# A hybrid decoder trunk on one core: the two halves of a norm's sum are added before the float32 product, and the planner's figures change

## The chip, the cores and the metric

The kernel runs on one core of a Trainium2 chip. The metric is device time in microseconds of one execution. The engines are named as in the profile: PE (TensorE matmuls), PEld (TensorE weight loads), DVE (VectorE), ACT (ScalarE), POOL (GpSimd) and SP (SyncE, which issues most DMAs).

## The reference, cut to what matters

Two layers act on a residual stream `h` of 528 tokens (16 meta tokens and 512 real ones) and 1024 channels. Each layer has a mixer and an FFN, each between two RMS norms:

```
def rms_norm(x, g):
    xf = x.astype(jnp.float32)
    y = xf * lax.rsqrt(jnp.mean(xf * xf, axis=-1, keepdims=True) + RMS_EPS)
    return (y * g.astype(jnp.float32)).astype(x.dtype)

def layer_norm(x, g, b):
    mu = jnp.mean(xf, axis=-1, keepdims=True)
    var = jnp.mean(jnp.square(xf - mu), axis=-1, keepdims=True)
    y = (xf - mu) * lax.rsqrt(var + LN_EPS)
...
for l in range(DEPTH):
    h = h + rms_norm(mixer(rms_norm(h)))      # attention, Conformer conv, short gated conv
    h = h + rms_norm(ffn(rms_norm(h)))        # up, causal conv, silu gate, down
```

The mixer has eight attention heads with a forget gate, a Conformer module of 256 channels (a causal convolution of 31 taps, a layer norm over its 256 channels, silu, a small product) and a short gated convolution. Their results get a norm per head and go through `w_out`.

## The kernel before, in words

**Layout.** Channels lie on the 128 partitions, tokens along the free dimension. A tensor of 1024 channels is 8 blocks (`KD`) of 128x528, and work goes by halves of 264 tokens (`hf` 0 and 1). In the last layer the first tokens are not needed, so there halves of 250 and 256 tokens occur.

**Products.** A weight is split into two float32r parts, `whi` and `wlo` (a cast on ACT, a subtraction on DVE, 128x1024 each), the activations too (`uhi`, `ulo` or the pairs `y`). `mm3` (L837) makes three products of these parts for each block; it is most of the kernel. The FFN's up projections run through L2288 where seven-term sums are used. Weights stream from DRAM all the time through `raw` tiles.

**Sums over channels.** A norm needs a sum over channels, thus over partitions. This is a product with a constant matrix in true float32: `om_d` (1/1024) for the RMS norms, `om_c` (1/256) for the layer norm, `bd` and `hsel` for the head norms. `Norms.square` squares two blocks at a time (ACT, L925) into a tile of two halves, 128x2x264; further pairs are added into the tile `acc` (DVE, L934). `Norms.factor` (L974) then multiplies `om_d` with each of the two halves and adds them up in PSUM. Some sums are kept apart: with `apart` the last two pairs of a sum are not added to `acc` but go to `om_d` as tiles `c` of their own, and `square_alone` (L950) squares a single block, for the very last norm. After the product come Ln (L984), Exp (L987), a square (L988) on ACT and two steps on DVE (L989, L995) that give the factor. `post_norm` scales the sub-layer's result (L1050), adds it to `h` (L1060) and makes the next activations (L1066 on ACT, L1068 on DVE).

**The layer norm** is in `conv_tail`: `om_c` with the two blocks of the convolution (tiles `cacc`, L1760), the subtraction of the mean, squares into the tiles `apad`, and `om_c` with both of those (L1789). The 31 taps before it (L1153) run on DVE.

**Attention.** For each head, L1593 makes logits for a row maximum, L1600 reduces them on DVE in pieces, L1608 puts the maxima on a diagonal on POOL (five pieces: one of 16 and four of 128), L1617 multiplies by ones, and the result goes into the row of `q` that the real logits (L1637) use. After Exp (ACT, L1644) POOL clears the part above the diagonal (L1651) and L1671 multiplies by the values. L1737 and L1323 are the products of the head norms.

**What sets the order.** In the mixers and in the norm stages (`finish`) a planner, the class `Flow`, deals all instructions out: each operation on ACT, DVE, POOL or SP has a duration (`us`), a priority, a delay until its result is there (`lat`) and the tokens it waits for; `flow.mm` advances TensorE's clock. The operation that can start first in this plan is issued next, so the plan's figures fix the order of each engine's queue; an engine then works through its queue in that order and waits where something is late. `act_us`, `dve_us` and `stt_us` give the durations. The FFN's products between these stages are not dealt out by the planner.

POOL also carries the accumulating DMAs of weight sums (L534), each of which waits for the one before.

Of the kernel before, what the change touches and what calls it, by code (L numbers as in the profile page):

```python
# [21 lines left out]
H = L // 2  # L22
# [339 lines left out]
def mm4_us(n):  # L362

    return max(n / 600 + 0.005, 0.22)


def act_us(n):
    return 0.17 + 0.0009 * n


def dve_us(n):
    return 0.17 + 0.00101 * n


def stt_us(n):
    return 0.22 + 0.00102 * n


def dma_us(n):
# [10 lines left out]
def tile_hybrid_trunk(ctx: ExitStack, tc: tile.TileContext, xT, wflat, pv_d, out):  # L390
# [97 lines left out]
    def half_sl(hf):  # L488
        return slice(H * hf, H * (hf + 1))
# [408 lines left out]
    class Norms:  # L898
# [17 lines left out]
        def square(self, key, k, src, n, *after, prio=1):  # L916

            apart = self.alone.get(key, self.apart.get(key[0], 0))
            s = self.sums.setdefault(key, {"parts": {}})
            us = act_us(2 * n)  # L920
            box, slot = {}, Slot()

            def squares(tile):
                box["c"] = tile()
                nc.scalar.activation(box["c"], src, AF.Square)  # L925

            if k == 0:
                a = act(us, lambda: squares(lambda: T(self.pool, [P, 2, H], F32, "acc", 2)[:, :, :n]), *after,
                        prio=prio, takes=[(self.acc, slot)])
                s["acc"], s["at"] = box, a  # L930
            else:
                a = act(us, lambda: squares(lambda: self.c_tile(n)), *after, prio=prio, takes=[(self.c, slot)])
                if k < KD - 2 * apart:
                    s["at"] = dve(dve_us(2 * n), lambda: nc.vector.tensor_add(s["acc"]["c"], s["acc"]["c"], box["c"]),  # L934
                                  a, s["at"], prio=prio)
# [65 lines left out]

    def gained(h, y, a, z, k, g, after, prio):

        return [act(act_us(z - a) + 0.06, lambda i=i: nc.scalar.activation(
            y[:, k + i, a:z], h[:, k + i, a:z], AF.Copy, scale=g[:, k + i:k + i + 1]), after, prio=prio) for i in range(2)]

    def pre_norm(norms, hf, n, hg, hg_at, out, at, prio):
# [16 lines left out]
    def post_norm(norms, key, nkey, h, h_at, a, z, yp, g, g_next, at, hf, prio, out_at, y_out, on_pe=(), to=None):  # L1024

        n = z - a
        yield from norms.factor(key, n)
        s = norms.sums[key]  # L1030
        sums = {}
        for k in on_pe:
            if k:
                slots = []
                for _ in range(2):
                    slots.append((yield from flow.grab(pring[0]["s"])))
                t = psum[:, 2:4]
            else:
                slots = [(yield from flow.grab(pring[0]["mm"]))]
                t = mmt(slots[0].buf)  # L1040
            for i in range(2):
                nc.tensor.matmul(t[:, i, :n], lhsT=ident, rhs=h[:, k + i, a:z], start=True, stop=False)
            flow.mm(2 * 0.0017 * n)
            sums[k] = t[:, :, :n], slots

        def pair(k, prio):
            y = yp[:, k:k + 2, a:z]
            hk = h[:, k:k + 2, a:z]
            if g is None:
                e = dve(dve_us(2 * n), lambda: nc.vector.tensor_mul(  # L1050
                    y, y, s["r"].unsqueeze(1).to_broadcast([P, 2, n])), s["r_at"], *y_out[hf, k], prio=prio)
            else:
                e = s["r_at"]
                for i in range(2):
                    e = dve(stt_us(n), lambda i=i: nc.vector.scalar_tensor_tensor(
                        y[:, i, :], in0=y[:, i, :], scalar=g[:, k + i:k + i + 1], in1=s["r"],
                        op0=ALU.mult, op1=ALU.mult), e, prio=prio)
            if k in on_pe:
                return e
            f = dve(dve_us(2 * n), lambda: nc.vector.tensor_add(hk, hk, y), e, *h_at, prio=prio)  # L1060
            if g_next is not None:
                at[hf, k] = []
                for i in range(2):
                    hi, lo = (uhi[:, k + i, a:z], ulo[:, k + i, a:z]) if to is None else (to[0][k + i], to[1][k + i])
                    gc = g_next[:, k + i:k + i + 1]
                    c = act(act_us(n) + 0.06, lambda i=i, hi=hi, gc=gc: nc.scalar.activation(  # L1066
                        hi, hk[:, i, :], AF.Copy, scale=gc), f, prio=prio)
                    at[hf, k] += [c, dve(stt_us(n), lambda i=i, hi=hi, lo=lo, gc=gc: nc.vector.scalar_tensor_tensor(  # L1068
                        lo, in0=hk[:, i, :], scalar=gc, in1=hi.bitcast(F32), op0=ALU.mult, op1=ALU.subtract), c, prio=prio)]
            if nkey is not None:  # L1070
                norms.square(nkey, k, hk, n, f, prio=prio)
            out_at[hf, k] = f
            return e

        scaled = [pair(k, prio + 0.01 * k) for k in range(0, KD, 2)]
        s["free"].close(*scaled)
        for k in on_pe:
            yield [scaled[k // 2]]
            t, slots = sums[k]
            for i in range(2):  # L1080
                nc.tensor.matmul(t[:, i], lhsT=ident, rhs=yp[:, k + i, a:z], start=False, stop=True)
# [43 lines left out]
    def mixer(l, ypool, first, close_first, spans, front, rzs, u_at):  # L1125
# [622 lines left out]
        def conv_tail(blk):  # L1748
# [4 lines left out]
            sq = [T(mq, [P, L + CK - 1], F32, "apad", 2) for _ in range(2)]  # L1753
            us, vs = act_us(H), dve_us(H)
            at = {}
            for hf in range(2):
                c = half_sl(hf)
                ps, slot = yield from bank("mm")
                for j in range(2):
                    nc.tensor.matmul(ps[:, :H], lhsT=om_c, rhs=conv[j][:, c], start=j == 0, stop=j == 1)  # L1760
# [10 lines left out]
            def silu(j, c, box, mine, e):  # L1771
# [9 lines left out]
                g = act(us, lambda: nc.scalar.copy(a2[j][0][:, c], n), f)  # L1781
                return dve(vs, lambda: nc.vector.tensor_sub(a2[j][1][:, c], n, a2[j][0][:, c].bitcast(F32)), g)

            for hf in range(2):
                c = half_sl(hf)
                yield [at[hf, 0], at[hf, 1]]
                ps, slot = yield from bank("mm")
                for j in range(2):
                    nc.tensor.matmul(ps[:, :H], lhsT=om_c, rhs=sq[j][:, c], start=j == 0, stop=j == 1)  # L1789
# [69 lines left out]
    def finish(norms, h, h_at, spans, ks, rhs, y_at, yp, gpost, gpre, nsplit, first=None, rz=None, scaled=None,  # L1859
# [13 lines left out]
        def evac(m, hf, src, tok, slot):  # L1873
            a, z = spans[hf]
            d = yp[:, m:m + 2, a:z]
            if merge:
                e = dve(dve_us(2 * n[hf]), lambda: nc.vector.tensor_add(d, d, src), tok, prio=0)
                slot.close(e)
                a = norms.square(("y", hf), m, d, n[hf], e, prio=0)
                y_out[hf, m] = [act(act_us(n[hf]) + 0.06, lambda i=i: nc.scalar.activation(  # L1880
                    d[:, i, :], d[:, i, :], AF.Copy, scale=gpost[:, m + i:m + i + 1]), a, prio=0.6 * hf) for i in range(2)] if GA else []
                return

            es = [act(act_us(n[hf]) + 0.06, lambda i=i: nc.scalar.activation(
                d[:, i, :], src[:, i, :], AF.Copy, scale=gpost[:, m + i:m + i + 1]), tok, prio=0) for i in range(2)]
            slot.close(norms.square(("y", hf), m, src, n[hf], tok, prio=0), *es)
            y_out[hf, m] = es
# [7 lines left out]
        def evac_alone(m, i, src, tok):  # L1895
# [5 lines left out]
            y_out.setdefault((hf, m), []).append(act(act_us(n[hf]) + 0.06, lambda: nc.scalar.activation(  # L1901
                d, d, AF.Copy, scale=gpost[:, m + i:m + i + 1]), b, prio=0.6))
            return e

# [124 lines left out]
    with tc.tile_pool(name="pre", bufs=2, reuse_waits="tile") as sp, tc.manual_schedule(engines=every):  # L2029
# [12 lines left out]
        reads = {}  # L2042
        for k in range(KD):
            hk, hi, lo, gc = h[:, k, :H], u_raw[0][k], u_raw[1][k], g0[:, k:k + 1]
            c = act(act_us(H) + 0.06, lambda hk=hk, hi=hi, gc=gc: nc.scalar.activation(hi, hk, AF.Copy, scale=gc),
                    h_at[0, k - k % 2], prio=0)
            d = dve(stt_us(H), lambda hk=hk, hi=hi, lo=lo, gc=gc: nc.vector.scalar_tensor_tensor(
                lo, in0=hk, scalar=gc, in1=hi.bitcast(F32), op0=ALU.mult, op1=ALU.subtract), c, prio=0)
# [442 lines left out]
```

## Time and profile before

| | us |
|---|---|
| median of 3 runs | 1262.84 |
| lowest and highest run | 1262.09, 1263.26 |
| the profiled execution: span from first to last instruction | 1262.4 |
| PE busy | 1243.7 |
| PEld busy | 1194.0 |
| DVE busy | 926.1 |
| ACT busy | 710.3 |
| POOL busy | 174.6 |

The profiled execution has no time of its own beside its span; the span lies 0.4 us under the median of the runs, which is taken as what lies around it. In a row of groups stand the line, the engine, the operation, out<-in, the count, then busy time and mean duration in ns, then the idle time of the engine just before and what ended it. In a row of the timeline stand the start in us from the span's start, the time taken, and in brackets the idle time before it. A wait row gives who waited for whom, the total in us, the number of times and the longest.

### The profile page before, as it was taken

The numbers are of one execution on the slowest core, as the hardware profiler recorded it, in microseconds if no ns is written. First come the engines' busy times: TensorE is split into PE (matmuls) and PEld (weight loads), VectorE is DVE, ScalarE is ACT, GpSimd is POOL, SyncE is SP. The second block draws the span as 40 slices with busy tenths as digits, with TensorE's granted clock in tenths as the row PEclk, the third lists the DMA queues.
The fourth block names the chain that finished last, engine by engine and source line by source line (L and its number), as shares of the span: only waits on it lengthen the run. The fifth ranks groups of instructions, "written<-read, shape, count | busy, mean of one in ns | idle before, by whom it ended". The sixth has DMA issues, their size and how long they took to land.

```text
span 1262.4 us, 24292 instructions
## 1 busy us (share of the span) xinstructions
PE 1243.7 (99%) x9554; PEld 1194.0 (95%) x9554; DVE 926.1 (73%) x1581; ACT 710.3 (56%) x1377; POOL 174.6 (14%) x360
## 2 busy tenths in 40 slices
PE   8999999999999999999999999999999999999997
PEld 8998898999999999999999988999999899989997
DVE  7887866589874776487688878656799748756964
ACT  7254576655444663476673545775554447526763
POOL 1323411001111001010003244120021000000000
PEclk9999999999999999999999999999999999999999
DMA  7357551726648755776652584547166565465611
GB/s 245 82 155 173 126 119 44 259 87 149 186 147 334 244 193 149 240 195 169 208 189 67 156 194 110 144 111 241 71 163 176 146 218 170 153 223 182 203 60 67
DMA packets 80755, 206.59 MB, mean 164 GB/s; under 512 B 8624, under 2 KB 18992, under 8 KB 80128
## 3 DMA queue, kind: packets, MB, share of 16 engines
q1 hardware_dynamic: 66976, 168.20, 42.1%
q0 software_dynamic: 13664, 36.84, 13.0%
q8 instruction: 75, 1.23, 0.4%
q14 instruction: 40, 0.33, 0.1%
HBM read 170.82 MB, written 50.60 MB: 175 GB/s over the span
## 4 chain that ended last, share of the span: by engine, by line
PE 89%; DVE 3%; issue 3%; DMA 2%; ACT 2%; POOL 1%; SPq 0%; DVEq 0%; POOLq 0%; ACTq 0%
PE psum L837 58%; PE psum L2288 17%; PE psum L1407 5%; PE psum L1671 3%; PE psum L1637 2%; PE psum L974 1%; PE psum L1593 1%; DMA raw<-in_w_dram 1%; PE psum L1737 1%; PE psum L1323 1%; DMA w_split<-slo 0%; DMA h<-in_w_dram 0%; POOL dm L1608 0%; DVE yp L1050 0%; DMA h<-in_x_dram 0%
## 5 line engine op out<-in xcount | busy, mean ns | idle before, releaser
L837 PE MATMUL psum<-y,whi 128*128 128x264 f32 (+3 forms) x1968 | 383.8, 299 | 0.8 <-DVE zs L989 0.7
L837 PEld LDWEIGHTS psum<-y,whi 128*128 128x128 f32 x1968 | 305.6, 188 | 13.8 <-DVE zs L989 0.9
L837 PE MATMUL psum<-uhi,whi 128*128 128x264 f32 (+1 forms) x1168 | 292.1, 289 | 1.5 <-ACT uhi L2069 0.7
L837 PE MATMUL psum<-ulo,whi 128*128 128x264 f32 (+1 forms) x1168 | 285.7, 284 | 0.6 <-DVE ulo L2071 0.4
L837 PE MATMUL psum<-uhi,wlo 128*128 128x264 f32 (+1 forms) x1168 | 285.1, 283 | 0.0
L837 PE MATMUL psum<-y,wlo 128*128 128x264 f32 (+3 forms) x984 | 273.7, 297 | 0.3 <-DVE wlo L793 0.3
L837 PEld LDWEIGHTS psum<-uhi,whi 128*128 128x128 f32 x1168 | 201.5, 188 | 6.2 <-issue 1.6
L837 PEld LDWEIGHTS psum<-ulo,whi 128*128 128x128 f32 x1168 | 201.6, 188 | 1.3 <-DVE ulo L2071 0.6
L837 PEld LDWEIGHTS psum<-uhi,wlo 128*128 128x128 f32 x1168 | 201.3, 188 | 0.0
L837 PEld LDWEIGHTS psum<-y,wlo 128*128 128x128 f32 x984 | 177.8, 188 | 5.8 <-DVE wlo L793 0.6
L2173 DVE SCALAR_TENSOR_TENSOR c<-zs,pv,c 128x528 f32<-128x528 f32 (+1 forms) x176 | 130.6, 756 | 23.5 <-ACT c L2171 22.2
L652 ACT CAST whi<-raw 128x1024 fp32r<-128x1024 f32 (+1 forms) x65 | 66.1, 1020 | 97.1 <-PE psum L837 74.5
L793 DVE TENSOR_TENSOR wlo<-raw,whi 128x1024 fp32r<-128x1024 f32 (+2 forms) x80 | 95.6, 1203 | 29.7 <-ACT whi L789 29.2
L789 ACT CAST whi<-raw 128x1024 fp32r<-128x1024 f32 (+2 forms) x80 | 81.7, 1031 | 24.9 <-PE psum L837 18.0
L653 DVE TENSOR_TENSOR wlo<-raw,whi 128x1024 fp32r<-128x1024 f32 (+1 forms) x65 | 76.9, 1183 | 21.1 <-ACT whi L652 21.0
L1153 DVE SCALAR_TENSOR_TENSOR cacc<-apad,pv,cacc 128x528 f32<-128x528 f32 x120 | 87.6, 772 | 0.1
L2288 PE MATMUL psum<-uhi,whi 128*128 128x258 f32 (+1 forms) x252 | 71.3, 284 | 0.0
L2288 PE MATMUL psum<-ulo,whi 128*128 128x258 f32 (+1 forms) x252 | 71.2, 283 | 0.0
L2288 PE MATMUL psum<-uhi,wlo 128*128 128x258 f32 (+1 forms) x252 | 70.7, 283 | 0.0
L2171 ACT ACTIVATE c<-zs,pv 128x528 f32<-128x528 f32 (+1 forms) x88 | 63.0, 727 | 6.8 <-DVE zs L2136 2.7
L2206 POOL COPY cols<-y 128x1 f32<-128x1 f32 x24 | 17.2, 716 | 335.8 <-ACT y L2187 335.5
L2288 PE MATMUL psum<-t,shi 128*128 128x258 f32 (+1 forms) x336 | 63.2, 283 | 0.0
(273 smaller groups left out, 2323.9 us busy)
## 6 DMA issues: line engine op xcount, KB each, us to landing
raw<-in_w_dram SPq DMA_DIRECT2D x114, 512.0 KB, 4.5
raw<-in_w_dram SPq DMA_DIRECT2D x30, 448.0 KB, 5.1
h<-in_w_dram SPq DMA_DIRECT2D x25, 512.0 KB, 4.5
raw<-w_sum SPq DMA_DIRECT2D x21, 512.0 KB, 5.4
h<-w_sum SPq DMA_DIRECT2D x21, 512.0 KB, 4.8
h<-in_w_dram POOLq DMA_DIRECT2D x16, 512.0 KB, 4.6
w_sum<-h POOLq DMA_DIRECT2D x16, 512.0 KB, 6.4
w_sum<-in_w_dram SPq DMA_DIRECT2D x26, 256.0 KB, 5.2
```

The source lines that it names most:

```text
L652: nc.scalar.copy(hi[:, :sz], raw[:, :sz])
L653: last_low[0] = nc.vector.tensor_sub(lo[:, :sz], raw[:, :sz], hi[:, :sz].bitcast(F32))
L789: nc.scalar.copy(box["hi"][:, :sz], box["raw"][:, :sz])
L793: nc.vector.tensor_sub(lo[:, :sz], box["raw"][:, :sz], box["hi"][:, :sz].bitcast(F32))
L837: nc.tensor.matmul(d, lhsT=w[a][:, k, cols], rhs=rhs(b, k, hf), start=start and i == 0 and p == 0, stop=stop and i == n - 1 and p == 2)
L1153: nc.vector.scalar_tensor_tensor(conv[j], in0=src, in1=conv[j], scalar=col("a_dw_w", CK * j + i), op0=ALU.mult, op1=ALU.add)
L1407: nc.tensor.matmul(ps[:n, :nw], lhsT=(uhi, ulo)[ui][:, k, P * b:P * b + n], rhs=w[wi][:, k % 4, :], start=k == 0 and p == 0, stop=k == KD ...
L1637: nc.tensor.matmul(s, lhsT=k[:, ka:ka + kn], rhs=q[:, s0:qz], start=i == 0, stop=i == 1)
L1671: nc.tensor.matmul(acc[:, s0 - qa:qz - qa], lhsT=vals[:, b].rearrange("p h d -> p (h d)")[:, o:o + P], rhs=box["p"], start=b == 0, stop=b ...
L2171: nc.scalar.activation(dst, src[:, 2:2 + 2 * fw], AF.Copy, scale=wtap(2, t))
L2173: nc.vector.scalar_tensor_tensor(dst, in0=src[:, i:i + 2 * fw], scalar=wtap(i, t), in1=dst, op0=ALU.mult, op1=ALU.add)
L2288: nc.tensor.matmul(psum[:, bank, :n7], lhsT=w[a][:, k0 + k, :], rhs=rhs(b, k), start=start and k == 0 and p == 0, stop=stop and k == K2 - ...
```

## The change

There are two edits. First, `Norms.fold` is new: it adds the second half of a squared tile to the first on DVE, and `factor` then makes one product instead of two; `square` calls it for `acc` and for the parts that are kept apart. `conv_tail` gets `both`, which adds the two blocks on DVE (into the first `apad` tile), so that each mean is one product by `om_c`. Second, the planner's figures: the durations of ACT and DVE get smaller, and each operation has a delay instead, 0.075 us on ACT and 0.06 on DVE.

```
 def act_us(n):
-    return 0.17 + 0.0009 * n
+    return 0.085 + 0.00085 * n
 def dve_us(n):
-    return 0.17 + 0.00101 * n
+    return 0.066 + 0.00105 * n
 def stt_us(n):
-    return 0.22 + 0.00102 * n
+    return 0.127 + 0.00105 * n
...
     def act(us, fn, *after, **kw):
-        return flow.op("act", us, fn, after, **kw)
+        return flow.op("act", us, fn, after, lat=0.075, **kw)
     def dve(us, fn, *after, **kw):
-        return flow.op("dve", us, fn, after, **kw)
+        return flow.op("dve", us, fn, after, lat=0.06, **kw)
...
                 s["parts"][max(0, k // 2 - KD // 2 + apart + 1) if k else 0] = box, slot
-                box["at"] = [a]
+                box["at"] = [self.fold(box, n, prio, a)] if k else [a]
             if k == KD - 2 * apart - 2:
-                s["acc"]["at"], s["acc"]["there"] = [s["at"]], True
+                s["acc"]["at"], s["acc"]["there"] = [self.fold(s["acc"], n, prio, s["at"])], True
             return a
+
+        def fold(self, box, n, prio, *after):
+
+            box["tiles"] = (0,)
+            return dve(dve_us(n), lambda: nc.vector.tensor_add(box["c"][:, 0, :], box["c"][:, 0, :], box["c"][:, 1, :]),
+                       *after, prio=prio)
...
+            def both(t, c, after):
+                return dve(vs, lambda: nc.vector.tensor_add(sq[0][:, c], t[0][:, c], t[1][:, c]), *after)
+
+            sums = [both(conv, half_sl(hf), taps) for hf in range(2)]
             for hf in range(2):
                 c = half_sl(hf)
+                yield [sums[hf]]
                 ps, slot = yield from bank("mm")
-                for j in range(2):
-                    nc.tensor.matmul(ps[:, :H], lhsT=om_c, rhs=conv[j][:, c], start=j == 0, stop=j == 1)
-                tok = flow.mm(2 * mm4_us(H))
+                nc.tensor.matmul(ps[:, :H], lhsT=om_c, rhs=sq[0][:, c], start=True, stop=True)
+                tok = flow.mm(mm4_us(H))
...
+            sums = [both(sq, half_sl(hf), [at[hf, 0], at[hf, 1]]) for hf in range(2)]
             for hf in range(2):
                 c = half_sl(hf)
-                yield [at[hf, 0], at[hf, 1]]
+                yield [sums[hf]]
                 ps, slot = yield from bank("mm")
-                for j in range(2):
-                    nc.tensor.matmul(ps[:, :H], lhsT=om_c, rhs=sq[j][:, c], start=j == 0, stop=j == 1)
-                box, mine, e = rsq(ps[:, :H], slot, LN_EPS, flow.mm(2 * mm4_us(H)))
+                nc.tensor.matmul(ps[:, :H], lhsT=om_c, rhs=sq[0][:, c], start=True, stop=True)
+                box, mine, e = rsq(ps[:, :H], slot, LN_EPS, flow.mm(mm4_us(H)))
```

Where an activation scales by a column, the planner's addition of 0.06 becomes 0.095. Because the figures change for every operation, the queues are dealt anew in all planned stages. Three places follow. Lines of the changed kernel are 6 to 11 higher than those before: L934 stays, the fold is L947, L989 becomes L995, L1153 becomes L1159, L1545 becomes L1551, L1593 becomes L1599, L1600 becomes L1606, L1617 becomes L1623, L1637 becomes L1643 and L1671 becomes L1677.

DVE at the opening, where the first half's squares are added up while weights are split (`acc_260` and `acc_231` are the first half's sums, `wlo` a split weight). Before:

```order
L793 TENSOR_TENSOR wlo_262<-raw_208,whi_253 128x1024
L934 TENSOR_TENSOR acc_260<-acc_260,c_269 128x528
L934 TENSOR_TENSOR acc_260<-acc_260,c_277 128x528
L793 TENSOR_TENSOR wlo_302<-raw_222,whi_288 128x1024
L934 TENSOR_TENSOR acc_260<-acc_260,c_300 128x528
L934 TENSOR_TENSOR acc_307<-acc_307,c_316 128x528
```

And in the changed kernel:

```order
L934 TENSOR_TENSOR acc_231<-acc_231,c_251 128x528
L793 TENSOR_TENSOR wlo_275<-raw_208,whi_259 128x1024
L934 TENSOR_TENSOR acc_231<-acc_231,c_270 128x528
L934 TENSOR_TENSOR acc_231<-acc_231,c_277 128x528
L793 TENSOR_TENSOR wlo_310<-raw_224,whi_291 128x1024
L947 TENSOR_TENSOR acc_231<-acc_231 128x264
L934 TENSOR_TENSOR acc_285<-acc_285,c_305 128x528
```

All three adds of the first half now stand ahead of the second of these splits, and only the fold stands behind it.

PE in the first layer's mixer, from the last matmul of the second head's maximum to the product with its diagonal (`dm`). Before:

```order
L1593 MATMUL psum_67<-k_84_698,q_92_706 128x264
L1637 MATMUL psum_67<-q_90_704,k_82_696 128x272
L1637 MATMUL psum_67<-q_91_705,k_83_697 128x272
L1671 MATMUL psum_67<-pf_1225,vals_681 128x400
L1637 MATMUL psum_67<-q_90_704,k_82_696 128x144
L1637 MATMUL psum_67<-q_91_705,k_83_697 128x144
L837 MATMUL psum_67<-uhi_108,whi_977 128x264
L837 MATMUL psum_67<-ulo_109,whi_977 128x264
L837 MATMUL psum_67<-uhi_108,wlo_986 128x264
L1671 MATMUL psum_67<-pf_1246,vals_681 128x272
L1617 MATMUL psum_67<-dm_99_730,ones_r_80 128x264 x2
```

And in the changed kernel:

```order
L1599 MATMUL psum_67<-k_84_698,q_92_706 128x264
L1677 MATMUL psum_67<-pf_1214,vals_681 128x400
L1643 MATMUL psum_67<-q_90_704,k_82_696 128x144
L1643 MATMUL psum_67<-q_91_705,k_83_697 128x144
L1677 MATMUL psum_67<-pf_1229,vals_681 128x272
L1623 MATMUL psum_67<-dm_99_730,ones_r_80 128x264 x2
```

Two logits and three products of the projections no longer stand between them.

DVE behind the last reduction of the third head in the first layer (`mcol` holds the maxima; the eleventh head, in the second layer, has the same rows with other numbers). Before:

```order
L1600 ISA mcol_1466 128x1
L1545 SCALAR_TENSOR_TENSOR pair_lo_1461<-psum_67,pair_hi_1460 128x264
L1600 ISA junk_1524,mcol_1466<-psum_67,causal_691,mcol_1466 128x264
L1600 ISA mcol_1466 128x1
L793 TENSOR_TENSOR wlo_1536<-raw_1180,whi_1517 128x1024
L793 TENSOR_TENSOR pw_1533<-raw_1478,pw_1533 128x512
```

And in the changed kernel:

```order
L1606 ISA mcol_1481 128x1
L1606 ISA junk_1528,mcol_1481<-psum_67,causal_691,mcol_1481 128x264
L1606 ISA mcol_1481 128x1
L1551 SCALAR_TENSOR_TENSOR pair_lo_1475<-psum_67,pair_hi_1474 128x264
L1159 SCALAR_TENSOR_TENSOR cacc_135<-apad_133,pv_3_69,cacc_135 128x528
L793 TENSOR_TENSOR wlo_1553<-raw_1216,whi_1533 128x1024
```

The subtraction `pair_lo`, which reads PSUM, moved behind the last reduction, and the weight split that stood there moved further back.

More of the change, by code (lines that the diff above doesn't have):

```diff
@@ L1002, in gained @@
     def gained(h, y, a, z, k, g, after, prio):
-        return [act(act_us(z - a) + 0.06, lambda i=i: nc.scalar.activation(
+        return [act(act_us(z - a) + 0.095, lambda i=i: nc.scalar.activation(
             y[:, k + i, a:z], h[:, k + i, a:z], AF.Copy, scale=g[:, k + i:k + i + 1]), after, prio=prio) for i in range(2)]
@@ L1065, in pair @@
                     gc = g_next[:, k + i:k + i + 1]
-                    c = act(act_us(n) + 0.06, lambda i=i, hi=hi, gc=gc: nc.scalar.activation(
+                    c = act(act_us(n) + 0.095, lambda i=i, hi=hi, gc=gc: nc.scalar.activation(
                         hi, hk[:, i, :], AF.Copy, scale=gc), f, prio=prio)
@@ L1900, in evac_alone @@
             b = norms.square_alone(("y", hf), 1 + i, d, n[hf], e, prio=0)
-            y_out.setdefault((hf, m), []).append(act(act_us(n[hf]) + 0.06, lambda: nc.scalar.activation(
+            y_out.setdefault((hf, m), []).append(act(act_us(n[hf]) + 0.095, lambda: nc.scalar.activation(
                 d, d, AF.Copy, scale=gpost[:, m + i:m + i + 1]), b, prio=0.6))
@@ L2044, in tile_hybrid_trunk @@
             hk, hi, lo, gc = h[:, k, :H], u_raw[0][k], u_raw[1][k], g0[:, k:k + 1]
-            c = act(act_us(H) + 0.06, lambda hk=hk, hi=hi, gc=gc: nc.scalar.activation(hi, hk, AF.Copy, scale=gc),
+            c = act(act_us(H) + 0.095, lambda hk=hk, hi=hi, gc=gc: nc.scalar.activation(hi, hk, AF.Copy, scale=gc),
                     h_at[0, k - k % 2], prio=0)
```

4 lines of the change are left out of this document (2 added, 2 removed).

## The prediction

> **What bounds the kernel now.** I read the page first: the busy shares, and the chain that ended last.
>
> ```profile
> PE 1243.7 (99%) x9554; PEld 1194.0 (95%) x9554; DVE 926.1 (73%) x1581; ACT 710.3 (56%) x1377; POOL 174.6 (14%) x360
> PE 89%; DVE 3%; issue 3%; DMA 2%; ACT 2%; POOL 1%; SPq 0%; DVEq 0%; POOLq 0%; ACTq 0%
> ```
>
> A busy share can hide gaps, since matmuls overlap. So I took the chain piece by piece; its longest piece is pure matmul.
>
> ```profile
> 277.08 107.95 PE psum L837 x886
> ```
>
> That is 0.122 us per matmul of 264 columns with nothing between them. TensorE is bound by its own instruction count there, and the view of TensorE's waits says it is so nearly everywhere:
>
> ```profile
> PE psum L1617 <- POOL dm L1608: 1.4, 2, 1.0
> PE psum L1081 <- DVE yp L1050: 1.4, 1, 1.4
> ...
> PE psum L974 <- ACT c L950: 1.0, 1, 1.0
> ...
> PE psum L1671 <- POOL pf L1651: 0.6, 2, 0.3
> PE psum L837 <- ACT uhi L1066: 0.5, 1, 0.5
> PE psum L974 <- DVE acc L934: 0.5, 1, 0.5
> ...
> PE psum L837 <- DVE ulo L1068: 0.3, 1, 0.3
> ```
>
> The view has 16 rows that sum to 13.1 us, about 1% of the span. So a TensorE instruction that goes away is time saved, unless it stood in one of these few waits.
>
> **What the change removes.** By the order of the instructions TensorE loses 28 matmuls of 9342 (both counts with the warm-up): 16 of `acc` and 4 of `c` by `om_d`, and 8 of the 16 by `om_c`. No other matmul is lost or added. One such float32 product is two records in the trace: the 16 `om_c` products of the program are 32 records.
>
> ```profile
> L974 PEld LDWEIGHTS psum<-acc,om_d 128*128 128x128 f32 x64 | 11.0, 189 | 1.6 <-issue 0.7
> L974 PEld LDWEIGHTS psum<-c,om_d 128*128 128x128 f32 x20 | 3.5, 189 | 1.6 <-ACT c L950 1.2
> L1760 PEld LDWEIGHTS psum<-cacc,om_c 128*128 128x128 f32 x16 | 2.9, 190 | 0.4
> L1789 PEld LDWEIGHTS psum<-apad,om_c 128*128 128x128 f32 x16 | 2.8, 190 | 0.3
> ...
> 162.50 1.78 PE psum L1760 x8
> 1247.76 1.29 PE psum L974 x6
> ```
>
> Eight records of 264 columns take 1.78 us: 0.2225 each, 0.445 us a product. Six of 256 take 1.29: 0.43 a product; for 250 columns I scale to 0.42. Removed are 24 products of 264, 2 of 256 and 2 of 250: 24 x 0.445 + 2 x 0.43 + 2 x 0.42 = **12.4 us** of TensorE time.
>
> **What it adds.** VectorE gets 28 adds of 128x264 float32 (a few of 250 or 256). Two adjacent rows of that shape give both of their prices.
>
> ```profile
> 27.70 0.43 DVE L1119 TENSOR_TENSOR sccx<-sccx,rz 128x264 f32<-128x264 f32 x1 [0.17 <-ACT sccx L1117]
> 28.06 0.43 DVE L1119 TENSOR_TENSOR cxp<-cxp,rz 128x264 f32<-128x264 f32 x1
> ```
>
> One starts 0.36 us after the other, and its result is there after 0.43. So 28 x 0.36 = 10.1 us more of VectorE time, and 0.43 us more until a sum may go to TensorE. In the chain of one norm the second nearly cancels: the add costs 0.43, the product that follows is 0.445 shorter. The VectorE time lies beside matmuls where VectorE has room:
>
> ```profile
> 130.00:162.00 32.00, 31.72 (x233) 27.85 (x232) 22.86 (x53) 17.50 (x49) 13.26 (x28) 1.00 0.46 108
> 162.00:190.00 28.00, 27.57 (x204) 26.22 (x203) 19.95 (x54) 22.93 (x59) 4.35 (x12) 1.00 0.52 125
> 620.00:677.00 57.00, 56.30 (x436) 55.02 (x436) 46.21 (x86) 39.06 (x85) 0.38 (x4) 1.00 0.48 168
> ```
>
> Columns are the length and the busy time of PE, PEld, DVE, ACT and POOL. The fullest stretch is 620 to 677, the end of the first FFN: 46.2 of 57 us, to which 8 adds bring 2.9. There is cover; if there were none, all 28 on the path would cost 10.1 us (a rival below). I take 0 for it.
>
> **Where the saving is lost.** At the opening the sum waits for a weight load:
>
> ```profile
> 14.91 1.05 ACT L789 CAST whi<-raw 128x1024 fp32r<-128x1024 f32 x1 [1.07 <-DMA raw<-in_w_dram]
> 16.00 1.23 DVE L793 TENSOR_TENSOR wlo<-raw,whi 128x1024 fp32r<-128x1024 f32 x1 [0.71 <-ACT whi L789]
> 17.14 2.13 DVE L934 TENSOR_TENSOR acc<-acc,c 128x528 f32<-128x528 f32 x3
> 17.99 1.13 PE L974 MATMUL psum<-acc,om_d 128*128 128x264 f32 x4 [0.47 <-DVE acc L934]
> ```
>
> In the order before, the last 528-wide add stands behind that L793. In the new order all three adds stand ahead of it and the fold alone behind it, so the product may start at about 17.14 + 0.43 + 0.1 = 17.7 instead of 17.99. The second half's fold stands behind a weight split and L995, and TensorE then arrives some 0.7 us earlier than before, so it may wait there. Two products, 0.89 us, are at stake; I count 0.4 lost, bounds 0 and 0.9. At the second mixer's end TensorE ran out of work (the rows on L1066 and L1068) while post_norm's chain ran, and one removed product of 250 columns stood there as cover: 0.4 lost, bounds 0 and 0.8. At the very end (the rows on L950 and L1081) the chain starts from the last matmul, which comes earlier by the whole saving; those sums were single tiles already. Nothing is lost.
>
> **The new order.** The planner's figures change for every act and dve operation, so in the mixers and the norm stages the queues are dealt anew. I looked where TensorE has the least room: the row maximum of a head goes matmul L1593, VectorE reduction L1600, POOL diagonal L1608, matmul L1617.
>
> ```profile
> 91.39 0.37 POOL L1608 TENSOR_SCALAR dm<-ident,mcol 128x128 fp32r<-128x128 f32 x1
> 91.96 0.60 PE L1617 MATMUL psum<-dm,ones_r 128*128 128x264 f32 x2
> ...
> 114.64 1.41 POOL L1608 TENSOR_SCALAR dm<-ident,mcol 128x128 fp32r<-128x128 f32 x1 [1.12 <-DVE mcol L1600]
> 114.64 1.26 DVE L793 TENSOR_TENSOR wlo<-raw,whi 128x1024 fp32r<-128x1024 f32 x1
> 116.11 0.39 PE L1617 MATMUL psum<-dm,ones_r 128*128 128x264 f32 x1 [0.44 <-POOL dm L1608]
> 142.20 0.82 POOL L1608 TENSOR_SCALAR dm<-ident,mcol 128x128 fp32r<-128x128 f32 x1 [0.86 <-DVE mcol L1600]
> ```
>
> The POOL step takes 0.37 us, but 1.41 when VectorE starts a weight split at the same instant. In the new order a different VectorE instruction follows that reduction (pair_lo, one input from PSUM) in both layers: up to 1.4 us of waits go, the whole of the first row of the waits. Against it, the second head now has two products and two logits between L1593 and L1617 where three L837 and two more logits stood besides: 5 x 0.122 = 0.6 less cover, with 91.96 - 91.76 = 0.2 to spare: 0.4 lost. And behind the last reduction of the first head of each layer now stands a convolution tap of two SBUF inputs; at 0.82 instead of 0.37 (the row at 142.20) that is 2 x 0.45 = 0.9. Together 0.1 lost. The promised delays are shorter throughout (0.403 for a 264-wide add, against 0.43 in the row), so I add 0.4 for many small waits: 0.5 for the order, bounds -6.5 (half of the listed waits gone) and +6.5 (as many again).
>
> The Trainium skill, page "SBUF — State Buffer", section "Who interferes with whom", says that a VectorE instruction with two SBUF inputs and a GpSimd instruction that reads SBUF exclude each other for a whole instruction. The rows at 114.64 agree. It speaks against the change, because all 28 adds have two SBUF inputs; 20 run where POOL has almost nothing to do (x4 in the 620 row), and the 8 of the convolution's layer norm beside POOL's masks could hold POOL for 8 x 0.43 = 3.4 us, by which the sum would be 1255.1. TensorE's waits for masks sum to 0.6 us in two places (the row on L1651), so I leave it out of the sum.
>
> **The sum.** The profiled span is 1262.4 and the median of the runs 1262.84; I take the 0.4 around the span as fixed. 1262.84 - 12.4 + 0.4 + 0.4 + 0.5 = **1251.7 us**.
>
> **Rivals.**
> 1. *More than the products.* The new order also takes half of the 13.1 us of waits: 1262.8 - 12.4 - 6.5 = 1244. For it speaks that the new figures fit the rows better (0.36 between starts, 0.343 in the planner, 0.437 before); against it, that most waits are ends of real chains. 0.08.
> 2. *VectorE becomes the bound.* The adds land in stretches where it runs back to back: up to 10.1 us given back, 1256 to 1261. The 11 us of room in the fullest stretch speak against it. 0.15.
> 3. *Slower: POOL's queue blocks a head.* The accumulating DMA L534 waits on POOL for an earlier transfer, and the heads' diagonals queue behind it.
>
> ```profile
> 65.59 0.89 POOL L534 DMA_DIRECT2D w_sum<-w_sum  x1 [6.42 <-DMA w_sum<-in_w_dram]
> ...
> 84.24 0.83 POOL L534 DMA_DIRECT2D w_sum<-w_sum  x1
> ...
> POOL w_sum L534 <- DMA w_sum<-in_w_dram: 26.9, 6, 6.4
> ```
>
> These waits stand now where no head is due. The new order puts one L534, the one at 84.24, between the third and the fourth of the first head's five diagonal pieces. It decides from two full waits (2 x 6.4 = 12.8 > 11.1); three give 1251.7 + 19.2 = 1271. Against it: the transfer that this one waits for is issued some 18 us earlier (65.59), and the issue alone takes 0.83. 0.08.
> 4. *No net change.* The order gives back as much as the products save, 1260.3 to 1265.4: 0.07.
>
> **How the numbers follow.** My forecast has 0.62, with 1248.5 to 1256 as its own range. About 0.2%, 2.5 us, is what a measurement can tell from no change. Faster by more: 0.62 + 0.08 + most of 0.15 = 0.84. Within: 0.07 and the rest of rival 2, 0.08. Slower: 0.08. The range leaves out rival 1, most of rival 3 and the edge of rival 2: 1247.5 to 1260.
>
> **What would show it.** L974's successor with 44 records instead of 84 and the `om_c` lines with 16 instead of 32; PE busy down by about 12 us with the waits still near 13; DVE busy up by about 10. The forecast is wrong if TensorE's waits grow by more than 4 us, on L1617's successor above all; rival 2 shows as waits on the adds or on L1050 and L1068's successors; rival 3 as POOL diagonals behind an L534.

## The result, and the profile after

The changed kernel takes 1278.37 us (median of 4 runs, 1275.74 to 1279.86) beside 1263.05 of the kernel before: a ratio of 1.0122, interval 1.0108 to 1.0136. It is slower by 15 us where 11 us faster were forecast. The 12.4 us of products are gone, so some 27 us came from elsewhere. The page of the changed kernel, the rows of the busy shares and of the chain by engine:

```profile
PE 1246.6 (98%) x9498; PEld 1186.9 (93%) x9498; DVE 932.7 (73%) x1609; ACT 709.5 (56%) x1377; POOL 180.9 (14%) x360
...
PE 76%; DVE 9%; ACT 5%; issue 4%; DMA 3%; POOL 1%; DVEq 0%; SPq 0%; ACTq 0%; POOLq 0%
```

56 records fewer are the 28 products, and yet PE's busy time is 2.9 us longer. That can't be work. A matmul's record lasts 0.28 us while the next one starts 0.122 us later, so a wait of up to some 0.16 us between two matmuls stays inside the busy time. The chain tells it: its share on PE fell from 89% to 76%.

Because busy time hides them, look for waits where they begin, at the weight loads. In the view of PEld's waits of the kernel before:

```profile
PEld psum L1617 <- POOL dm L1608: 2.3, 4, 1.2
...
PEld psum L1593 <- issue: 1.4, 1, 1.4
```

and of the changed kernel:

```profile
PEld psum L1599 <- issue: 5.2, 4, 4.2
PEld psum L1677 <- POOL pf L1657: 4.2, 12, 0.8
PEld psum L1599 <- DVE mcol L1606: 4.2, 13, 0.7
...
PEld psum L1800 <- DVE pair_lo L1551: 3.0, 2, 1.5
PEld psum L1599 <- DMA k<-pair_hi: 2.3, 1, 2.3
```

TensorE now waits twelve times for a mask from POOL, thirteen times for VectorE to finish a row maximum that holds a PSUM bank, twice in the layer norm, and 4.2 and 2.3 us for `k` of the second head. PE's own view of waits sums to 24.5 us (13.1 before), the weight loads' view the many small ones besides.

Where the time went is a sum over all matmuls: the distance from each start to the next, less what that matmul takes back to back (0.122 us for 264 columns, 0.2225 for one record of a float32 product). It holds waits and time at a lower clock alike (1.7 us of the latter in the changed kernel, see the last section). This is worked out from the records of each trace; the differences between kernels come out as their spans have them, within 0.2 us (57.6 - 29.9 - 12.4 = 15.3 for the changed kernel, whose span grew by 15.4).

| us of TensorE beyond its matmuls | before | changed | adds hidden | 5 ns less | 5 ns more | longer busy |
|---|---|---|---|---|---|---|
| 0 to 65, opening | 5.3 | 6.3 | 7.0 | 6.1 | 6.0 | 6.3 |
| 65 to 225, first mixer | 7.1 | 17.2 | 8.9 | 11.0 | 6.7 | 9.7 |
| 225 to 690, norms and first FFN | 1.5 | 6.0 | 4.8 | 1.5 | 3.4 | 8.8 |
| 690 to 860, second mixer | 7.4 | 19.4 | 8.1 | 12.4 | 16.7 | 10.4 |
| 860 to the end | 8.6 | 8.8 | 10.0 | 6.9 | 8.6 | 9.3 |
| sum | 29.9 | 57.6 | 38.8 | 37.9 | 41.4 | 44.6 |

(The last four columns are experiments below.) Of the 27.7 us that the changed kernel adds, 22 lie in the two mixers, where the planner deals out everything. The largest single piece, in the timelines of the kernel before and of the changed one (TensorE's last matmul before the second head's first logits in the second layer, these logits, and SP's issue of a weight load and of that `k`):

```profile
736.38 0.28 PE L837 MATMUL psum<-uhi,wlo 128*128 128x264 f32 x1
737.79 0.34 PE L1593 MATMUL psum<-k,q 128*16 128x16 f32 x2 [1.12 <-DMA k<-pair_hi]
...
728.57 0.47 SPq L785 DMA_DIRECT2D raw<-in_w_dram  x1
...
733.49 2.39 SPq L1499 DMA_DIRECT2D k<-pair_hi  x4
```

```profile
746.66 0.28 PE L837 MATMUL psum<-uhi,wlo 128*128 128x264 f32 x1
751.01 0.34 PE L1599 MATMUL psum<-k,q 128*16 128x16 f32 x2 [4.07 <-issue]
...
742.29 0.75 SPq L785 DMA_DIRECT2D raw<-in_w_dram  x1
743.78 4.08 SPq L1505 DMA_DIRECT2D k<-pair_hi  x4
```

In both, the issue of the four transfers begins 2.9 us ahead of TensorE's last matmul. Before, it takes 2.39 us and the logits start 1.9 us behind its end; in the new order it takes 4.08 and they start 3.1 us behind it. There a weight load was issued 1.5 us ahead of `k` (4.9 us before), which may be what slows it; that was not tried by itself.

### The profile page after: what moved, and what is told of

The parts are those of the page before. It is cut to its first block, busy times and chain, and to the rows that moved or that the text cites. A ratio compares the mean times of both kernels' runs of the same rounds, so it can differ in the third digit from the quotient of the medians.

```text
span 1277.8 us, 24199 instructions
## 1 busy us (share of the span) xinstructions
PE 1246.6 (98%) x9498; PEld 1186.9 (93%) x9498; DVE 932.7 (73%) x1609; ACT 709.5 (56%) x1377; POOL 180.9 (14%) x360
## 4 chain that ended last, share of the span: by engine, by line
PE 76%; DVE 9%; ACT 5%; issue 4%; DMA 3%; POOL 1%; DVEq 0%; SPq 0%; ACTq 0%; POOLq 0%
PE psum L837 50%; PE psum L2299 17%; PE psum L1413 4%; PE psum L1677 2%; ACT whi L789 1%; PE psum L1643 1%; DVE junk L1606 1%; DVE ulo L1074 1%; DVE wlo L793 1%; DVE yp L1056 1%; DVE h L1066 1%; PE psum L1599 1%; DVE acc L934 1%; PE psum L1743 1%; DMA raw<-in_w_dram 1%
## 5 line engine op out<-in xcount | busy, mean ns | idle before, releaser
L837 PE MATMUL psum<-uhi,whi 128*128 128x264 f32 (+1 forms) x1168 | 295.8, 291 | 3.3 <-ACT zs L2384 1.1
L1159 DVE SCALAR_TENSOR_TENSOR cacc<-apad,pv,cacc 128x528 f32<-128x528 f32 x120 | 86.9, 766 | 0.3
L2217 POOL COPY cols<-y 128x1 f32<-128x1 f32 x24 | 21.9, 913 | 322.3 <-ACT y L2198 322.0
```

Of the source, the lines that this page charges most:

```text
L837: nc.tensor.matmul(d, lhsT=w[a][:, k, cols], rhs=rhs(b, k, hf), start=start and i == 0 and p == 0, stop=stop and i == n - 1 and p == 2)
L1159: nc.vector.scalar_tensor_tensor(conv[j], in0=src, in1=conv[j], scalar=col("a_dw_w", CK * j + i), op0=ALU.mult, op1=ALU.add)
L2217: t = nc.gpsimd.tensor_copy(ticks, src.bitcast(F32))
```

## Experiments

Each time stands beside runs of the kernel before on the same chip; ratios have 95% intervals.

### Adds or figures?

Theory P: the new figures alone cost the 27 us. Theory V: the adds do. Theory R: any new deal does. The first run is the change without its second edit (`act_us`, `dve_us`, `stt_us`, the delays and the 0.06 as before), the second is the kernel before with the second edit alone.

> All adds as in the changed kernel, but the planner's figures of before (whole durations, no delay). Theory P (the loss of 27 us that eats the 12 us of products comes from the new figures alone): the products' 12 us stay saved, 1250 to 1255. Theory V (the adds on VectorE themselves cost it): as the changed kernel, 1272 to 1280. Theory R (any new deal of the queues costs, since the order of before was a lucky one): the adds change the plan too, so 1257 to 1270.

> The kernel before with its 28 products, only the planner's new figures. Theory P: the loss without the saving, 1263 + 22 to 28 = 1285 to 1291. Theory V: no adds, so no loss, 1260 to 1266. Theory R: a loss of 5 to 25 whose size is not foretold, 1268 to 1288.

Measured: 1273.32 (1.0086, 1.0066 to 1.0107) and 1286.47 (1.0186, 1.0171 to 1.0201). The figures alone cost 23.5 us, as P says (R's range holds it too), and V falls, since that run has no add. Its trace has the changed kernel's waits all the same: the weight loads wait 5.8 us for masks (5.7 in the changed kernel), 2.8 us for VectorE's `pair_lo` (3.0) and 2.0 us for `k` (2.3). But with the old figures the adds don't gain 10 us, they lose 11: P falls as the whole story. Two more runs, each with one engine's figures as before and the other's split:

> The changed kernel with ScalarE's figures of before; VectorE's stay split into busy time and delay. Theory P, with VectorE as the culprit (in 40 to 120 us it is busy 36 of 40 us, so a plan with too short VectorE steps lets urgent steps stand late): nearly the whole loss, 1272 to 1280. Theory P with ScalarE as the culprit: 1250 to 1256. Theory V: 1272 to 1280.

> The changed kernel with VectorE's figures of before; ScalarE's stay split into busy time and delay. Theory P with VectorE as the culprit: nearly all of the loss gone, 1250 to 1257. Theory P with ScalarE as the culprit: 1272 to 1280. Theory R: both halves lose something, each 1258 to 1272.

Measured: 1279.62 (1.0128, 1.0110 to 1.0146) and 1281.55 (1.0154, 1.0137 to 1.0171). Either split alone gives the whole loss; neither engine is the culprit.

### The same order with and without the adds

So the order has to be held fixed. Here the planner is told nothing (it charges two products and no add), and each add is issued right behind the instruction that makes its input. ACT, POOL and SP keep their order to the instruction, PE loses 24 products, DVE gains 24 adds:

```
+                    def add():
+                        t = s["acc"]["c"]
+                        nc.vector.tensor_add(t, t, box["c"])
+                        if k == KD - 2 * apart - 2:
+                            nc.vector.tensor_add(t[:, 0, :], t[:, 0, :], t[:, 1, :])
+                            s["acc"]["tiles"] = (0,)
+
+                    s["at"] = dve(dve_us(2 * n), add, a, s["at"], prio=prio)
```

> The order of before, kept: 24 of the 28 products (16 by om_d, 8 by om_c) become single ones, each add is issued right behind the VectorE instruction that makes its input (in the layer norm's second sum behind ScalarE's squares), and the planner is told nothing: it charges the old figures and two products. Only the 4 products of tiles c stay double. Theory R (before's order was a good one, and any new deal of the queues costs 20 us or more): 24 x 0.445 = 10.7 us are saved and stay saved, 1251 to 1255. Theory V (the adds cost as much as they save, by VectorE's time or by the longer chain in front of the product): 1260 to 1275.

Measured: 1262.77 beside 1263.86 (0.9994, 0.9984 to 1.0003). The time lies in V's range, yet both theories lose a part: the changed kernel is 15.6 us slower with four products fewer, so its order costs that much, as R says; but of the 10.7 us of products only about 1 is left (-0.4 to 2.0). Why, shows the second sum of the layer norm. The kernel before, TensorE:

```profile
164.72 0.29 PE L837 MATMUL psum<-uhi,wlo 128*128 128x264 f32 x1
164.85 1.05 PE L1789 MATMUL psum<-apad,om_c 128*128 128x264 f32 x4
```

The kernel with the adds hidden, VectorE and then TensorE:

```profile
164.42 1.22 DVE L793 TENSOR_TENSOR wlo<-raw,whi 128x1024 fp32r<-128x1024 f32 x1
165.55 0.43 DVE L1764 TENSOR_TENSOR apad<-apad,apad 128x264 f32<-128x264 f32 x1
...
164.59 0.28 PE L837 MATMUL psum<-uhi,wlo 128*128 128x264 f32 x1
166.03 0.71 PE L1800 MATMUL psum<-apad,om_c 128*128 128x264 f32 x2 [1.16 <-DVE apad L1764]
```

Before, these products needed only ScalarE's squares and started behind the last matmul. Now they need VectorE too, in whose queue a weight split stands: 1.16 us of waiting for 2 x 0.2225 saved. Its waits that name an add:

```profile
PE psum L1800 <- DVE apad L1764: 2.3, 2, 1.2
...
PE psum L980 <- DVE acc L938: 1.4, 2, 0.8
```

Two more runs take this apart in the same order: the products single and no adds, so that each of these sums leaves out half of its channels; and all products double with 20 adds whose result nobody reads. Of the edits, the lines for the sums over `acc`, against the run with the adds hidden:

```
-                            nc.vector.tensor_add(t[:, 0, :], t[:, 0, :], t[:, 1, :])
```

```
+                            nc.vector.tensor_add(box["c"][:, 0, :], t[:, 0, :], t[:, 1, :])
```

> The order of before, the 24 products single, and no adds at all: each of these sums leaves out half of its channels, so the factors are not the norms' (the same instructions run on them). Theory C (the products are saved, and what the adds give back is their place in the chain, sum to add to product): 1251 to 1255, so that the adds cost some 9 us. Theory W (TensorE waits after those products anyway, so that taking them away saves little): 1257 to 1263.

> The order of before with all products double, and 20 of the 24 adds issued on VectorE at the places of the run with the adds hidden from the plan, into a tile that nobody reads (the 4 of the layer norm's second sum are left out). Only VectorE's time is added. Theory C: it lies beside matmuls, 1262 to 1265. Theory Q (VectorE's queue is what the adds lengthen: 20 x 0.36 = 7.2 us, most of it on the path): 1267 to 1271.

Measured: 1256.58 beside 1263.37 (0.9943, 0.9929 to 0.9956) and 1264.17 (1.0002, 0.9993 to 1.0011). VectorE's time costs nothing that can be measured, though it is busy 7.6 us longer:

```profile
PE 1243.6 (99%) x9554; PEld 1193.3 (95%) x9554; DVE 933.7 (74%) x1601; ACT 710.5 (56%) x1377; POOL 175.7 (14%) x360
```

Theory Q falls, as far as these 20 adds go (the four of the layer norm's second sum are not among them). Of the 10.7 us of products 7.2 (5.6 to 9.0) are saved where no add follows; the other 3.5 were cover in front of waits (2.8 by the spans of the two traces, 1262.4 and 1254.5). And 7.2 less the 0.8 that stay with the adds (up to 2.0) leaves some 6 us as the price of the add's place: between a sum and its product, on a second engine's queue. The time of the first run lies between the ranges of C and W: C is right in kind, W for a third of the products.

### Keeping the part that pays

> As the run with the adds hidden from the plan, but the layer norm keeps its double products: 16 folds alone. By the traces of that run its 8 layer norm products gave back all that they saved (+0.2 us in each layer), so 1262.8 - 0.4 = 1261 to 1263.5 if the rest repeats; 1256 to 1259 if the two waits at weight loads (1.1 us at 9 us, 1.0 us at 424 us) were chance.

> The order of before with 20 single products, the adds hidden from the plan and off the chain: the sum is folded before its last pair of squares arrives, which is then added in two steps of 264 columns (0.36 + 0.43 us) where 528 columns and a fold took 0.6 + 0.43; of the layer norm only the first sum is added. Theory C (place in the chain): the chain of a norm becomes shorter than before, so most of 20 x 0.445 = 8.9 us stays saved, 1254 to 1259. Theory W or Q: 1260 to 1264.

The first leaves the layer norm's products double. The second folds the sum ahead of its last pair, then adds the pair in two steps, and keeps only the layer norm's first add:

```
+                        if k == end and k > 2:
+                            for i in range(2):
+                                nc.vector.tensor_add(t[:, 0, :], t[:, 0, :], box["c"][:, i, :])
+                        else:
+                            nc.vector.tensor_add(t, t, box["c"])
+                            if k == max(2, end - 2):
+                                nc.vector.tensor_add(t[:, 0, :], t[:, 0, :], t[:, 1, :])
```

Measured: 1260.94 (0.9985, 0.9976 to 0.9995) and 1261.15 (0.9978, 0.9968 to 0.9988). Both beat the kernel before, by 2 to 3 us of 7.1 and 8.9 us of products. The shorter chain did not bring the 4 to 9 us that C expected; the time lies where W or Q had it. Its waits are spread over the ends of the norms; which of them take the rest, and so how much of the 6 us is the length of the chain, was not settled.

### What is bad about the new order?

If any deal costs, a change of 5 ns in VectorE's two constants of before must cost as well.

> The kernel before, every product as it was; only the planner's constants for VectorE are 5 ns lower (0.165 and 0.215). No step gets a truer or a falser figure by it that could matter. Theory R: the queues are dealt anew in some 80 places and that alone costs, 1268 to 1285. Theory P (what costs is the split into busy time and delay): 1260 to 1266.

> As the run before, with 5 ns more (0.175 and 0.225). Theory R: 1268 to 1285. Theory P: 1260 to 1266.

Measured: 1271.97 (1.0064, 1.0049 to 1.0079) and 1275.58 (1.0092, 1.0075 to 1.0109), 8 and 12 us for a figure that nothing in the chip knows of. The table shows it as chance: with 5 ns more the first mixer is as good as before (6.7), the second 9 us worse. Its largest wait, of TensorE:

```profile
PE psum L1617 <- DVE rs_t L1292: 3.8, 2, 3.3
```

Both lie in R's range: the order of before is better than that of either neighbour. Then the split figures themselves, moved by 5 ns, and with longer delays (`lat` 0.125 and 0.11):

> The changed kernel with delays of 0.125 us on ScalarE and 0.11 on VectorE in place of 0.075 and 0.06, so that the plan never promises a result before it is there (0.453 us for a 264-wide add, 0.43 measured). Theory P' (promised too early): about half of the 27 us or more come back, 1252 to 1266. Theory R: another deal like the rest, 1270 to 1284.

> The changed kernel with VectorE's constants 5 ns lower (0.061 and 0.122): a neighbour of its order, dealt anew in about 80 places. Theory R (chance of the deal alone): it scatters as the deals of the old figures did, anywhere from 1262 to 1285, one of the two neighbours below 1274 or above 1283. Theory F (the split figures themselves deal worse, by what they promise): close to the changed kernel, 1275 to 1282.

> The changed kernel with VectorE's constants 5 ns higher (0.071 and 0.132). Theory R and theory F as for the run with 5 ns less.

Measured: 1280.68 (1.0131, 1.0111 to 1.0152), 1278.58 (1.0117, 1.0100 to 1.0134) and 1276.76 (1.0102, 1.0087 to 1.0117). With the two half splits that makes six deals of split figures with the adds, all within 1276.8 to 1281.6 (that range counts the changed kernel itself). The three new deals of the whole figures so far lay at 1272.0 to 1275.6, although two of them keep all products double (12.4 us); without the adds, the split figures took 1286.5. That is hardly chance alone and supports theory F, that the split figures deal worse, though only one deal of the whole figures has all the adds (1273.3). Longer delays don't mend it (P' falls). Next, the wait for `k`; the plan alone is told that the transfers of `q` and `k` land later (`lat=2.2` to `lat=3.6`), in the changed kernel and, as a control, in the one before:

> The changed kernel; the plan alone promises the transfers of q and k 1.4 us later (0.6 + 3.6 us from the start of the issue where it said 0.6 + 2.2; the traces show 2.4 to 5.3 us from issue to landing). Theory K (the split lets the second head's row maximum be dealt ahead of its k, and TensorE waits 2.1 us in the first and 4.1 us in the second layer for it): these two waits go, 1270 to 1274. Theory R: they go, and other waits come in their place, 1275 to 1283.

> The control: the kernel before with the same later promise for q and k. Theory K: its waits for k were 1.2 and 1.1 us, they go, 1260 to 1264. Theory R: the order of before is lost, 1268 to 1280.

Measured: 1275.11 (1.0081, 1.0059 to 1.0104) and 1261.29 (0.9984, 0.9975 to 0.9994). In the control the waits for `k` are gone, with a gain of 1.9 us: there K is right. R, which had 1268 to 1280 for it, is wrong: 46 of VectorE's 1581 instructions stand elsewhere than before (137 and 118 in the runs with 5 ns less and more), and nothing is lost. So most new deals cost, but not every one. In the changed kernel one of the waits for `k` stays at 2.4 us and others grow: 3 to 5 us of 15 come back, in R's range and just outside K's. Last, longer busy times with the delays kept, so that the plan gives VectorE about a tenth more than it takes (the old figures gave a fifth):

```
-    return 0.066 + 0.00105 * n
+    return 0.096 + 0.00115 * n
```

> The changed kernel with its delays kept and longer busy times: 0.096 + 0.00115 n on VectorE (0.400 us for 264 columns, where two adds start 0.36 apart) and 0.115 + 0.00095 n on ScalarE, so that the plan gives both engines a tenth more than they take, as the old figures did. Theory M (the old figures' margin is what the split took away): 1266 to 1274, with the sum of TensorE's small waits in the mixers down. Theory F without margin (the split as such): 1275 to 1283.

Measured: 1266.85 (1.0029, 1.0018 to 1.0040). Groups of weight loads of the changed kernel (masks times values, logits of the maximum, the same for a block of 16):

```profile
L1677 PEld LDWEIGHTS psum<-pf,vals 128*128 128x128 f32 x160 | 24.5, 189 | 6.6 <-POOL pf L1657 4.2 <-issue 0.8 <-ACT yta L1691 0.6
...
L1599 PEld LDWEIGHTS psum<-k,q 128*128 128x128 f32 x80 | 15.1, 192 | 5.4 <-DVE mcol L1606 4.2 <-ACT whi L789 0.3 <-issue 0.2
...
L1599 PEld LDWEIGHTS psum<-k,q 128*16 128x16 f32 x16 | 1.5, 96 | 7.3 <-issue 5.0 <-DMA k<-pair_hi 2.3
```

and with longer busy times:

```profile
L1677 PEld LDWEIGHTS psum<-pf,vals 128*128 128x128 f32 x160 | 24.6, 188 | 4.6 <-POOL pf L1657 2.7 <-ACT yta L1691 1.2
...
L1599 PEld LDWEIGHTS psum<-k,q 128*128 128x128 f32 x80 | 14.9, 188 | 0.8
...
L1599 PEld LDWEIGHTS psum<-k,q 128*16 128x16 f32 x16 | 1.5, 96 | 0.2 <-issue 0.2
```

The waits for the maxima (4.2 us) and for `k` (7.3 us) are gone, and the mixers stand at 9.7 and 10.4 us in place of 17.2 and 19.4. That is what theory M asks for: the old figures gave VectorE 0.437 us for an add that takes 0.36 between starts, the new ones 0.343, and a queue that is planned faster than it runs would be late everywhere by a little.

Three things keep M from being shown. The old figures leave more room still, and with them the planned adds took 1273.32. One deal may be luck, where 5 ns moved the time by 8 and 12 us. And in this deal one head norm's sum in each layer is overwritten in its PSUM bank by the product of the short convolution's norm before ScalarE and VectorE read it, so that norm comes out wrong. In the first layer the overwriting product starts at 199.2 us and the reads meant for the sum end at 204.5, in the second at 830.6 and 835.9: a plan that kept the bank could lose up to 2 x 5.3 us, nearly all of the 11.5 us by which this run is faster than the changed kernel. M is a candidate; why the split figures deal worse stays open.

At the end the two edits that gained, together:

> The two edits that gained alone, together: the early folds hidden from the plan, in the order that the plan of before makes with the later landing of q and k. If they add: 1263.2 - 2.2 - 1.9 = 1259, range 1257.5 to 1261. If both take the same waits: 1260.5 to 1262.

Measured: 1259.37 beside 1263.34 (0.9967, 0.9955 to 0.9979). The gains add within the noise, and this is the best version: 4 us under the kernel before, 19 under the changed one.

## Why the prediction was wrong

- *The products (12.4 us).* Counted rightly: 56 records fewer. A group of the sums over `acc`, of the changed kernel (64 records before):

```profile
L980 PEld LDWEIGHTS psum<-acc,om_d 128*128 128x128 f32 x32 | 4.9, 188 | 0.9 <-DVE acc L947 0.7
```

- *VectorE's time (0).* Right: adds that nobody waits for cost 0.3 us by the ratio of 1.0002, and 1.4 us at the end of its interval.
- *"In the chain of one norm the second nearly cancels".* This is the first step that failed. It was taken as a reason that the chain isn't longer, while the full 0.445 per product stayed on the list of savings. Where a product stands at the end of a chain, the add in front of it takes the saving back, and the queue it stands in can take more. Only two places were priced, at 0.8 us together; in the order of before some 10 of 10.7 us came back, 3.5 of them as cover lost in front of waits and some 6 by the adds' place. Of the two places that were priced, neither lost anything on balance in the changed kernel (0.4 forecast for each). The opening as a whole lost 1.0 us, but not at the norm's sum: TensorE's 0.5 us in front of the first half's product are gone, the weight loads wait 0.3 for the second half's fold, and TensorE's waits for a split weight grew from 0.3 to 1.0. At the second mixer's end the waits on L1066 and L1068 sum to 0.8 before, on their successors to 0.7.
- *The new order (0.5, bounds -6.5 and +6.5).* The second step that failed, and the larger one. Forecast at 0.5 us, it measured 15.6 between the adds in the two orders (28 and 24 of them), and 23.5 where the figures were changed alone. It was priced at the one place where TensorE waited most, and there it was right: the POOL diagonal's 1.4 us are gone from the waits. But in an order whose waits sum to 1%, nearly every pair of instructions is a place that can get worse, and few can get better; symmetric bounds from "half of the waits" were the wrong form. The +0.4 "for many small waits" had the right sign and was far too small. Rival 1 counted it for the new figures that 0.343 lies nearer to 0.36 than 0.437 does; that it lies below may be what is bad about them (theory M), which is not shown.
- *The rivals.* Rival 3 ended on the right side by a mechanism that did not occur (no diagonal waits behind an L534). Rival 2's 10.1 us were refuted by the unread adds. "No net change" was too near: the order gives back more than twice what the products save.
- *POOL and two SBUF inputs.* Leaving out the 3.4 us was right: POOL is busy 175.6 us with the adds hidden (174.6 before), and the masks' wait stays 0.6 us there. In the changed kernel the weight loads wait 5.7 us for masks, but with the figures alone, without an add, 5.8. The Trainium skill, page "SBUF — State Buffer", section "Who interferes with whom", has the exclusion; no run here shows that it cost these adds anything.
- *What would show it.* "Wrong if TensorE's waits grow by more than 4 us" did flag it: they grew by 11, and some 16 more of the 27.7 us lie in what PE's view doesn't show. But on L1617's successor, where the sign was to show above all, PE's view shows no wait any more.

## What to carry to other kernels

Price an instruction that is removed by what waits behind it: at the end of a dependency chain, replacing half of it by work on another engine can save next to nothing (here 0.8 of 10.7 us, with the queue's order unchanged). Where a planner deals the queues, hold the order fixed to measure an edit, and move a figure by 5 ns to learn how far chance goes (here 8 to 12 us); only then is an effect of the edit told from one of the deal. Look for the loss at the weight loads and in start-to-start distances: TensorE can wait in many places, each too short to be seen in its busy share. Busy times planned a little above what the engines take may deal better; one run points that way, and it shows no more than that.

## What the runs showed that was not expected

The 4.35 us between the two matmuls at 746.66 and 751.01 also cost clock. The changed kernel by stretches of 5 us (after the five engines: granted clock, DMA share, GB/s):

```profile
745.00:750.00 5.00, 1.95 (x17) 1.74 (x15) 2.05 (x3) 0.39 (x1) 0.52 (x1) 1.00 1.06 250
750.00:755.00 5.00, 3.99 (x20) 4.02 (x21) 2.20 (x9) 0.00 (x0) 1.78 (x4) 0.66 0.73 186
755.00:760.00 5.00, 5.00 (x42) 4.76 (x41) 4.30 (x13) 3.70 (x9) 1.09 (x4) 1.00 0.53 121
```

The granted clock is 0.66 over the 5 us in which TensorE starts again, so 0.34 x 5 = 1.7 us of work are lost on top of the pause; after the pause of 1.4 us in the kernel before it stays at 1.00. The Trainium skill, page "TensorE: Matmul & The Clock Gate", section "What's actually happening", has half the clock after an idle window of about 3.4 us and full clock after one busy window; an estimate from that, 3.4 us at half clock, is the same 1.7 us, which agrees.

The length of one pause does not decide it, though. In the run with VectorE's constants of before 5 ns lower, a single pause of 2.2 us between two starts was enough (half the clock from 744.0 to 747.4 us). In the run with `lat` 0.125 and 0.11 one of 3.1 us (at 111.2 us) brought no loss of clock, nor did one of 3.4 us (at 661.9) in the changed kernel with 5 ns more. So the half clock's length is as the page has it, but an idle window of 3.4 us was not its condition in these runs, and the measurements decide. A long wait can thus be dearer than it looks, here by 1.7 us on 4.1; from which length on, these runs don't say.
